# A hand-laid order for four engines in the opening of a gated mLSTM and differential-attention block, with in-bank output gates and the remainders of q and k on GpSimd

## The chip, the cores and the metric

The kernel runs on one core of one Trainium2 chip. The metric is the device time of one execution in microseconds (us). The median of three runs of the kernel before is 1762.96 us (1762.74 to 1768.04). A difference of about 0.3%, some 5 us, is what a measurement of this kernel can tell from none.

## The reference

One block over a sequence of 1024 tokens of width 1024, in fp32. The parts that matter here:

```python
h = rmsnorm(x, norm_g)
proj = h @ w_in                       # 11 segments of 1024 columns and one of 16
(a_q, a_k, a_v, a_o, a_z, a_g, b_q, b_k, b_v, b_z, g_a, g_b) = split(proj)
qk = silu(centred_depthwise_conv(concat(a_q, a_k), conv_w))     # 5 taps
h_fw, h_bw = mlstm(mq, mk, mv, gates from a_g), the same reversed
y_a = rmsnorm(h_fw + h_bw) * sigmoid(a_o) * silu(a_z)           # "output gates"
y_b = rmsnorm(diff_attention(rope(b_q), rope(b_k), b_v)) * silu(b_z)
mix = sigmoid(g_a + gb[0]) * (y_a @ w_branch_a) + sigmoid(g_b + gb[1]) * (y_b @ w_branch_b)
out = rmsnorm(x + mix @ w_out) * final_g
```

## The kernel before, in words

**Number format.** Every large product is made from two fp32r parts, a rounded high part `H` and a remainder `L = value - H`, with three matmuls (H·H, H·L, L·H). Making a pair of parts costs a copy on ScalarE (ACT) and a subtraction on VectorE (DVE) or GpSimd (POOL). TensorE (PE) has the most work of all engines.

**Opening** (from `begin`, L1417, to `leave("p0")`). Eight tiles of x (128 tokens by 1024) are loaded on the SP queue: x0 to x3, the raw weights of the first gate block, x4 to x7, the next weights. `load_small` (L442) loads `norm_g` and `gate_b` on ACT's queue; `gate_b` arrives transposed by the DMA, element by element, as `gbh` [128, 16]. `norm_x` (L486) makes the sum of squares on ACT (L491), the power -1/2 on POOL (L141), and on DVE the small steps around it (L138 to L145) and the scaling of the tile (L493). PE transposes x0 to x3 into eight PSUM banks (L130; two of tag `pj`, six of tag `T`). `split_h` makes `hH` (ACT, L537) and `hL` (DVE, L538). Then come gate blocks g0 to g3: each is a column block of 128 for two halves of the tokens, 24 matmuls of 128x512 per half (L408), finished by a tanh on ACT (`gt`, L761) that empties one of the two `pj` banks. Their weights are split by `load_w` (ACT L197, then eight POOL subtractions L200). Between them PE transposes x4 to x7 (`transpose_x`), and `first_part` (`f`, ACT L508) and `sums` (L510 to L525) make four sums of h blocks (`t`, `f` on DVE L516, L519 and POOL L520, L521) and their parts `TH` (ACT L524) and `TL` (DVE L525). The sums are operands of the next stage.

**Pairs.** Sixteen pairs of column blocks of w_in follow, alternately one of k or q (with the convolution) and one of the output gates a_o and a_z. A pair takes seven products f0 to f6 of 12 matmuls each instead of eight (L277); `load_form` makes the weight form of each product (POOL L233, L238, ACT L254, and the remainder L256 on DVE for f0, f4, f6, on POOL for the rest). Products land in `T` banks, of which there are six in turn; sums (`u`, L280) and the sinks on DVE free them. `conv_sink` adds the product into `cin` (L339), runs the five taps in a bank (L353, L355), tanh (`tz`, L356), silu (`y`, L358), the high part (ACT L361) and the remainder (DVE L364), and stores the parts. `oz_sink` adds the product into an SBUF tile `oz` (L314), takes tanh (L316, L319), multiplies the halves (L320), and at last multiplies the two tiles of 1024 columns (L325). The gates of the mLSTM (`gch`, DVE) and the rope angles (`wk`) are made beside pairs 1 to 8.

After the pairs (from 424 us on in the profile) come attention, the mLSTM and the output products. The change leaves the order of instructions there as it was.

**What sets the order.** PE keeps the order in which the program is written. For ACT, DVE, POOL and SP a scheduler fixes each engine's order when the kernel is built, from its own estimate of costs; on the chip each engine then runs its list strictly in order and waits at the first instruction that is not ready.

Of the kernel before, what the change touches and what calls it, by code (L numbers as in the profile page):

```python
# [109 lines left out]
class Block:  # L110
    def __init__(self, tc, A):
        self.tc, self.nc, self.A = tc, tc.nc, A
        nc = self.nc
        self.v, self.a, self.p, self.t, self.q = nc.vector, nc.scalar, nc.gpsimd, nc.tensor, nc.sync
        self.wt = {}
        self.raws = {}
        self.ml, self.opening, self.terms = False, True, {}
        for n in ("w1", "w2", "wy", "wr"):
            setattr(self, n, _Late(self, "_" + n))
        self.gc = {}  # L120
# [50 lines left out]
    def load_w(self, key):  # L171
        if key in self.wt:
            return
        if key[0] == "sw":
            return self.load_form(key)
# [83 lines left out]
    def pair_units(self, p, sink):  # L259
# [9 lines left out]
        def product(f, k0):  # L269
# [20 lines left out]
            elif f == 3:  # L290
                sink(1, 1, ps, box["u3"])
                add(box["u2"], box["u2"])
# [12 lines left out]
    def oz_sink(self, i0):  # L305

        v, a, box = self.v, self.a, {}

        def sink(i, j, ps, rest):
            if i not in box:  # L310
                box[i] = (self.big("oz"), [])
            t, got = box[i]
            c = slice(j * 512, (j + 1) * 512)
            v.tensor_tensor(out=t[:, c], in0=ps, in1=rest, op=ALU.add)  # L314
            if i == 0:
                a.activation(out=t[:, c], in_=t[:, c], func=AF.Tanh, scale=0.5)  # L316
            else:
                th = self.s0.tile([128, 512], F32, name="tz", tag="tz", bufs=2)
                a.activation(out=th, in_=t[:, c], func=AF.Tanh, scale=0.5)  # L319
                v.scalar_tensor_tensor(out=t[:, c], in0=th, scalar=1.0, in1=t[:, c], op0=ALU.add, op1=ALU.mult)  # L320
            got.append(j)
            if len(got) < 2 or len(box) < 2 or any(len(g) < 2 for _, g in box.values()):
                return
            o, z = box[0][0][:, 0:S], box[1][0][:, 0:S]
            v.scalar_tensor_tensor(out=z, in0=o, scalar=1.0, in1=z, op0=ALU.add, op1=ALU.mult)  # L325
            self.q.dma_start(out=self.gd_ml[i0], in_=z)
        return sink

    def conv_sink(self, seg, n):
# [3 lines left out]
        def sink(i, j, ps, rest):  # L333
# [12 lines left out]
            for half in range(2):  # L346
# [17 lines left out]
                v.tensor_tensor(out=lo.bitcast(F32R), in0=yh, in1=H, op=ALU.subtract)  # L364
# [3 lines left out]
    def run(self, units):  # L368
# [10 lines left out]
        for i, u in enumerate(units):  # L379
            if u.keys:  # L380
# [3 lines left out]
                while nxt < len(order) and (order[nxt][0] != "sw" or hasattr(self, "_s0")) and (nxt < need or nxt <= need + (4 if order[nxt][0] == "sw" else 1) and room(order[nxt])):  # L384
                    self.load_w(order[nxt])
                    nxt += 1
# [55 lines left out]
    def load_small(self, pool):  # L442
        A, q = self.A, self.a
        self.gin = pool.tile([8, 128], F32, name="gin")
        q.dma_start(out=self.gin, in_=A["norm_g"].rearrange("o (t c) -> (o t) c", c=128))
        self.gbh = self.const.tile([128, 16], F32, name="gbh")
        q.dma_start(out=self.gbh, in_=A["gate_b"].rearrange("o g (t c) -> c (o g t)", c=128))
# [13 lines left out]
    def norm_gain(self):  # L461
        ps = self.bank("T")
        self.tr(ps[:, 0:8], self.gin)
        self.g_in = self.const.tile([128, 8], F32, name="g_in")
        self.v.tensor_copy(self.g_in, ps[:, 0:8])

# [19 lines left out]
    def norm_x(self, pool, i):  # L486

        x = self.xs[i]
        ssq = pool.tile([128, 1], F32, name="ssqx", bufs=2)
        sq = pool.tile([128, D], F32, name="sq", tag="sq", bufs=2)  # L490
        self.a.activation(out=sq, in_=x, func=AF.Square, accum_out=ssq)  # L491
        rs = self.rsqrt(pool, ssq, 1.0 / D, EPS, f"rs{i}", bufs=2)
        self.v.tensor_scalar(out=x, in0=x, scalar1=rs[:, 0:1], scalar2=None, op0=ALU.mult)  # L493
# [16 lines left out]
    def sums(self, pool, k, half):  # L510

        v, p, fb = self.v, self.p, lambda x: x.bitcast(F32)
        f, ps, g = self.f[k], self.xps[k + 4 * half], self.g_in[:, k + 4 * half:k + 4 * half + 1]
        if half == 0:
            self.t12 = t = pool.tile([128, D], F32, name="t12", tag="sq", bufs=2)
            v.scalar_tensor_tensor(out=t[:, 0:512], in0=ps, scalar=g, in1=f[:, 0], op0=ALU.mult, op1=ALU.subtract)  # L516
            return
        t1, t2 = self.t12[:, 0:512], self.t12[:, 512:1024]
        v.scalar_tensor_tensor(out=t2, in0=ps, scalar=g, in1=t1, op0=ALU.mult, op1=ALU.subtract)  # L519
        p.tensor_tensor(out=f[:, 0], in0=t2, in1=f[:, 0], op=ALU.subtract)  # L520
        p.tensor_tensor(out=f[:, 1], in0=f[:, 1], in1=t2, op=ALU.subtract)  # L521
        t = (t1, t2, f[:, 0], f[:, 1])
        for i in (1, 0, 2, 3):
            self.a.copy(self.TH[i][:, k], t[i])  # L524
            v.tensor_tensor(out=self.TL[i][:, k], in0=t[i], in1=fb(self.TH[i][:, k]), op=ALU.subtract)  # L525
# [847 lines left out]
    def build(self):  # L1373
# [21 lines left out]
        with pool(name="const", bufs=1) as self.const, \  # L1395
                pool(name="dram", bufs=1, space=bass.MemoryType.DRAM) as self.dram, \
                pool(name="psA", bufs=1, space=bass.MemoryType.PSUM) as self.psA, \
                pool(name="wts", bufs=1) as wp, \
                tc.manual_schedule(engines={mybir.EngineType.PE}):
# [20 lines left out]
            def begin():  # L1420
# [4 lines left out]
                keys = [g[0].keys[0] for g in (g0, g1)]  # L1425
# [7 lines left out]
                for i in range(4):  # L1433
                    self.norm_x(self.p0, i)
                self.load_w(keys[0])
# [6 lines left out]
                  enter("p0", "p0", side="right"), banks("ps0", T=6), do(begin))  # L1442
# [4 lines left out]
            w.add(*[do(lambda i=i: self.transpose_block(i), 8 * TP) for i in range(4)])  # L1447
            first = lambda a, b: [self.first_part(self.p0, j) for j in range(a, b)]
# [116 lines left out]
```

## Time and profile before

| | value |
|---|---|
| median of three runs | 1762.96 us |
| the profiled execution's own time | 1767.53 us |
| its span, first to last instruction | 1765.8 us |
| PE busy | 1669.9 us (95%) |
| PE busy up to 86.52 us, where the pairs begin | 59.0 us |
| PE busy in the pairs, 86.52 to 424 us | 320.5 of 337.5 us |
| DVE, POOL busy in the pairs | 296.2 us, 177.1 us |
| granted TensorE clock: opening, pairs, the rest | 0.94, 0.97, 0.99 |

Time outside the span is 1.7 us. A granted clock of 0.94 over 86.5 us means that 0.06 of that stretch was lost to a slower clock. "Idle before" in a row is the time its engine stood still just ahead of it, and the name behind the arrow is what ended that.

### The profile page before, as it was taken

The numbers are of one execution on the slowest core, as the hardware profiler recorded it, in microseconds if no ns is written. First come the engines' busy times: TensorE is split into PE (matmuls) and PEld (weight loads), VectorE is DVE, ScalarE is ACT, GpSimd is POOL, SyncE is SP. The second block draws the span as 40 slices with busy tenths as digits, with TensorE's granted clock in tenths as the row PEclk, the third lists the DMA queues.
The fourth block names the chain that finished last, engine by engine and source line by source line (L and its number), as shares of the span: only waits on it lengthen the run. The fifth ranks groups of instructions, "written<-read, shape, count | busy, mean of one in ns | idle before, by whom it ended". The sixth has DMA issues, their size and how long they took to land. (4 is left out here: it accounts for less than half of the span.)

```text
span 1765.8 us, 24827 instructions
## 1 busy us (share of the span) xinstructions
PE 1669.9 (95%) x9119; PEld 1426.4 (81%) x9119; DVE 1064.3 (60%) x1957; ACT 769.9 (44%) x1522; POOL 568.6 (32%) x576
## 2 busy tenths in 40 slices
PE   4998998999999999999999989989999989999998
PEld 3777776788878888798789878889999877878886
DVE  3779989887156666666666755425666743225533
ACT  5544544444245554445445444424655643122211
POOL 3654654553331423312441331222321311222000
PEclk9999999999999999999999999999999989999999
DMA  5243434343634523451535162156454327344222
GB/s 153 84 130 103 137 108 131 108 143 120 145 94 108 142 62 82 126 134 43 145 94 132 47 151 67 61 158 188 136 163 148 100 75 251 122 140 134 84 84 84
DMA packets 191484, 208.15 MB, mean 118 GB/s; under 512 B 14681, under 2 KB 137954, under 8 KB 191362
## 3 DMA queue, kind: packets, MB, share of 16 engines
q1 hardware_dynamic: 188418, 204.98, 39.9%
q10 hardware_dynamic: 2944, 1.59, 0.3%
q8 instruction: 72, 1.18, 0.3%
q14 instruction: 50, 0.41, 0.1%
HBM read 143.47 MB, written 63.05 MB: 117 GB/s over the span
## 5 line engine op out<-in xcount | busy, mean ns | idle before, releaser
L408 PE MATMUL pj<-hH,wH 128*128 128x512 f32 x640 | 260.5, 407 | 14.4 <-ACT f L508 4.6
L408 PE MATMUL pj<-hH,wL 128*128 128x512 f32 x640 | 254.3, 397 | 0.1
L408 PE MATMUL pj<-hL,wH 128*128 128x512 f32 x640 | 253.8, 397 | 0.1
L853 ACT ACTIVATE e<-S,nm 128x1024 f32<-128x1024 f32 x128 | 143.1, 1118 | 179.1 <-DVE nm L851 178.8
L202 POOL TENSOR_TENSOR wL<-raw,wH 128x1024 fp32r<-128x1024 f32 x41 | 99.8, 2434 | 319.1 <-ACT wH L197 319.1
L874 DVE TENSOR_TENSOR pL<-T,pH 128x512 fp32r<-128x512 f32 x128 | 88.0, 687 | 139.9 <-ACT pH L873 139.8
L851 DVE TENSOR_REDUCE nm<-S 128x1 f32<-128x1024 f32 x128 | 155.8, 1217 | 20.2 <-PE S L849 20.0
L408 PEld LDWEIGHTS pj<-hH,wH 128*128 128x128 f32 x640 | 123.0, 192 | 38.9 <-ACT f L508 4.8
L430 PE MATMUL pj<-wH,hH 128*128 128x256 f32 x512 | 148.5, 290 | 0.2
L430 PE MATMUL pj<-wL,hH 128*128 128x256 f32 x512 | 145.9, 285 | 1.4 <-POOL wL L200 1.4
L430 PE MATMUL pj<-wH,hL 128*128 128x256 f32 x512 | 145.5, 284 | 0.0
L408 PEld LDWEIGHTS pj<-hH,wL 128*128 128x128 f32 x640 | 122.2, 191 | 27.9 <-POOL wL L187 0.9
L408 PEld LDWEIGHTS pj<-hL,wH 128*128 128x128 f32 x640 | 122.8, 192 | 23.4 <-DVE hL L538 0.6
L408 PE MATMUL pj<-sl_yb,wH 128*128 128x512 f32 x384 | 124.3, 403 | 4.1 <-ACT sl_yb L1258 2.0
L197 ACT CAST wH<-raw 128x1024 fp32r<-128x1024 f32 x56 | 58.7, 1052 | 125.3 <-PE pj L408 112.9
L430 PEld LDWEIGHTS pj<-wL,hH 128*128 128x128 f32 x512 | 98.5, 192 | 2.3 <-POOL wL L200 2.3
L430 PEld LDWEIGHTS pj<-wH,hH 128*128 128x128 f32 x512 | 98.7, 193 | 1.6 <-ACT wH L197 0.6
L430 PEld LDWEIGHTS pj<-wH,hL 128*128 128x128 f32 x512 | 98.5, 192 | 0.9
L355 DVE SCALAR_TENSOR_TENSOR T<-cin,cols,T 128x512 f32<-128x512 f32 x128 | 90.2, 752 | 7.3 <-ACT T L353 7.1
L849 PE MATMUL S<-kst,qH 128*128 128x512 f32 x256 | 89.7, 430 | 4.1 <-DMA kst<-stk 4.1
L860 DVE SCALAR_TENSOR_TENSOR e<-e,r,e 128x1024 f32<-128x1024 f32 x64 | 92.6, 1447 | 1.3
L408 PEld LDWEIGHTS pj<-sl_yb,wH 128*128 128x128 f32 x384 | 73.3, 191 | 24.5 <-DVE sl_yb L1259 3.2
(356 smaller groups left out, 4201.6 us busy)
## 6 DMA issues: line engine op xcount, KB each, us to landing
raw<-in_w_in_dram SPq DMA_DIRECT2D x88, 512.0 KB, 3.8
stk<-hl SPq DMA_DIRECT2D x64, 256.0 KB, 3.7
qH<-stk SPq DMA_DIRECT2D x32, 256.0 KB, 4.7
qL<-stk SPq DMA_DIRECT2D x32, 256.0 KB, 5.0
kst<-stk SPq DMA_DIRECT2D x16, 512.0 KB, 4.1
x<-in_x_dram SPq DMA_DIRECT2D x8, 512.0 KB, 3.8
cak<-y SPq DMA_DIRECT2D x16, 256.0 KB, 2.1
cakH<-cin SPq DMA_DIRECT2D x16, 256.0 KB, 2.0
```

The source lines that it names most:

```text
L197: self.a.copy(wH, raw)
L202: self.p.tensor_tensor(out=wL, in0=raw, in1=wHf, op=ALU.subtract)
L355: v.scalar_tensor_tensor(out=acc, in0=raw[:, o + x:o + x + 512], scalar=w(x), in1=acc, op0=ALU.mult, op1=ALU.add)
L408: self.t.matmul(ps, lhsT=l[:, k, :], rhs=r, start=(n == 0), stop=(n == 23))
L430: self.t.matmul(ps[:, i, :], lhsT=l, rhs=r[:, k, :], start=(kh == 0 and k == 0 and m == 0), stop=(kh == 1 and k == 3 and m == 2))
L849: self.t.matmul(ps[:, o], lhsT=x[:, j, c], rhs=st["k"][:, j, o], start=first, stop=not first)
L851: v.tensor_reduce(out=nm, in_=ps, axis=AX.X, op=ALU.max, negate=True)
L853: a.activation(out=e, in_=ps, func=AF.Exp, bias=nm[:, 0:1], accum_out=Z[:, j, t:t + 1])
L860: v.scalar_tensor_tensor(out=e0, in0=e, scalar=r[:, 0:1], in1=e0, op0=ALU.mult, op1=ALU.add)
L874: v.tensor_tensor(out=pL[:, :, s], in0=ps, in1=pH[:, :, s].bitcast(F32), op=ALU.subtract)
```

## The change

1. **Order.** `keep(PE, ACT, DVE, POOL)` holds all four engines to the written order from the start to the end of the opening; `keep(PE)` then hands ACT, DVE and POOL back to the scheduler. The units of the opening are written anew: the normalisation is cut into `norm_a` (squares, mean, power), `norm_b` (one Newton step, now two DVE instructions) and `norm_c` (scaling by two columns in one instruction), the sums into `sums_a`, `sums_b`, `sums_l`. Weight loads stand at fixed places (`ld`), and the look-ahead in `run` is off in the opening.
2. **gate_b.** It is loaded as 16 rows of 128 beside `norm_g` and turned by PE in the same transpose; the halving of `gbh` moves to `norm_gain`, just behind it.
3. **oz_sink.** The product is added in its PSUM bank, tanh reads the bank, and one SBUF tile `oz` per pair takes the product of the halves; each half is stored by itself.
4. **conv_sink.** The remainder of q and k (32 subtractions of 128x512) moves from DVE to POOL.

```diff
 def oz_sink (per product, i: 0 is a_o, 1 is a_z; j: half)
-            v.tensor_tensor(out=t[:, c], in0=ps, in1=rest, op=ALU.add)
+            v.tensor_tensor(out=ps, in0=ps, in1=rest, op=ALU.add)
+            more = lambda out, x, y: v.scalar_tensor_tensor(out=out, in0=x, scalar=1.0, in1=y, op0=ALU.add, op1=ALU.mult)
             if i == 0:
-                a.activation(out=t[:, c], in_=t[:, c], func=AF.Tanh, scale=0.5)
+                a.activation(out=z if first else ps, in_=ps, func=AF.Tanh, scale=0.5)
+                if not first:
+                    more(z, ps, z)
             else:
-                a.activation(out=th, in_=t[:, c], func=AF.Tanh, scale=0.5)
-                v.scalar_tensor_tensor(out=t[:, c], in0=th, scalar=1.0, in1=t[:, c], op0=ALU.add, op1=ALU.mult)
-            v.scalar_tensor_tensor(out=z, in0=o, scalar=1.0, in1=z, op0=ALU.add, op1=ALU.mult)
-            self.q.dma_start(out=self.gd_ml[i0], in_=z)
+                a.activation(out=th, in_=ps, func=AF.Tanh, scale=0.5)
+                more(z if first else ps, th, ps)
+                if not first:
+                    more(z, z, ps)
 def conv_sink
-                v.tensor_tensor(out=lo.bitcast(F32R), in0=yh, in1=H, op=ALU.subtract)
+                p.tensor_tensor(out=lo.bitcast(F32R), in0=yh, in1=H, op=ALU.subtract)
 def load_small
-        q.dma_start(out=self.gbh, in_=A["gate_b"].rearrange("o g (t c) -> c (o g t)", c=128))
+        q.dma_start(out=self.gin[8:24], in_=A["gate_b"].rearrange("o g (t c) -> (o g t) c", c=128))
 def build
-                tc.manual_schedule(engines={mybir.EngineType.PE}):
+            w.add(..., keep(E.PE, E.Activation, E.DVE, E.Pool), do(begin))
-            w.add(*g0[:k], *g1[:k], *[tx[i] for i in (0, 4, 1, 5, 2, 6)], sums[0])
-            w.add(*g2[:k], tx[3], tx[7], *g0[k:], do(lambda: (self.params(), self.lam(self.p0))), *[sums[i] for i in (1, 2, 3)])
-            w.add(*g1[k:], *g2[k:])
+            w.add(nA(0), nB(0), nC(0), tb(0), nA(1), nB(1), nA(2), nC(1), tb(1), nB(2), nA(3), nC(2), tb(2), nB(3), nC(3), tb(3))
+            w.add(ld(0), sp(0), fp(0), *[sp(i) for i in range(1, 8)], fp(1), nA(4), ld(1), nA(5), *g0[:k])
+            w.add(nB(4), nC(4), nA(6), nB(5), nC(5), nA(7), ld(2), fp(2, 3, 4, 5, 6, 7), nB(6), nC(6), nB(7), nC(7), *g1[:k])
+            w.add(*g2[:4], tx(0, 4, 1, 5), *g2[4:6], sA(0), tx(2, 6), *g2[6:k])
+            w.add(*g0[k:k + 4], tx(3, 7), sB((0, 1)), *g0[k + 4:k + 7], sB((0, 0)), sA(1), sL((0, 2), (0, 3)), g0[k + 7])
+            w.add(sB((1, 1), (1, 0)), sA(2), sL((1, 2), (1, 3)), ld(3), *g1[k:], sB((2, 1), (2, 0)), sA(3), sL((2, 2), (2, 3)))
+            w.add(*g2[k:], sB((3, 1), (3, 0)), sL((3, 2), (3, 3)), do(lambda: (self.params(), self.lam(self.p0))), keep(E.PE))
```

How the lists of three engines change at the places of which the prediction speaks. First DVE at the very start, before the change; `gbh` is the gate bias, `rs_v`, `rs_w`, `rs_y` the small columns of the normalisation, `x` a tile:

```order
L1415 MEMSET mhalf 128x8
L1451 TENSOR_SCALAR gbh<-gbh 128x16
L138 TENSOR_SCALAR rs_v<-ssqx 128x1 x2
L142 TENSOR_TENSOR rs_w<-rs_y 128x1 x2
L465 COPY g_in<-T 128x8
L143 TENSOR_TENSOR rs_w<-rs_w,rs_v 128x1 x2
```

The same place on DVE after the change:

```order
L1455 MEMSET mhalf 128x8
L473 COPY g_in<-T 128x8
L474 TENSOR_SCALAR gbh<-T 128x16
L502 TENSOR_SCALAR rsv<-ssqx 128x1
L509 SCALAR_TENSOR_TENSOR rsv<-rsy,rsv 128x1
L510 TENSOR_SCALAR rsv<-rsv 128x1
L514 TENSOR_SCALAR x_182<-x_182,rsy,rsv 128x1024
```

The halving of `gbh` stood at the head of DVE's list, ahead of all of the normalisation, and waited for the element-wise DMA; now the head waits for PE's transpose of 24 rows, and tile x0 is scaled before any other tile is begun.

Then ACT from the first split to the first tanh, before the change (`sq` are squares of x4 to x7, `f` the copies for the sums, `wH` high parts of weights):

```order
L491 ACTIVATE sq,ssqx<-x_200 128x1024
L491 ACTIVATE sq,ssqx<-x_202 128x1024
L508 ACTIVATE f<-T,g_in 128x512 x6
L197 CAST wH<-raw 128x1024 x2
L761 ACTIVATE gt<-pj,gbh 128x512
```

The same stretch of ACT after the change:

```order
L529 ACTIVATE f<-pj,g_in 128x512
L501 ACTIVATE sq,ssqx<-x_195 128x1024
L199 CAST wH<-raw 128x1024
L501 ACTIVATE sq,ssqx<-x_197 128x1024
L790 ACTIVATE gt<-pj,gbh 128x512
```

The weights of g1 now come behind one square instead of behind all squares and six copies `f`.

At last POOL in pair 0 (k) and pair 1, after the change; `tz` and `y` are the moved remainders, the rest makes weight forms:

```order
L240 TENSOR_TENSOR s1f<-raw 128x512
L369 TENSOR_TENSOR tz<-y,cin 128x512 x2
L258 TENSOR_TENSOR wH<-s2f,wH 128x512
L235 TENSOR_TENSOR s2f<-s1f,raw 128x512
L369 TENSOR_TENSOR tz<-y,cin 128x512 x2
L258 TENSOR_TENSOR wL<-s2f,wL 128x512
```

Before, the same list had no L369 rows; four subtractions that wait for DVE's `y` and ACT's copy now stand between the steps that make weight forms for PE.

123 lines of the change are left out of this document (73 added, 50 removed).

## The prediction

> **What bounds the kernel now.** I read the page first, then PE's waits up to the end of the pairs, then busy time by stretches, then the timeline around each wait.
>
> ```profile
> span 1765.8 us, 24827 instructions
> PE 1669.9 (95%) x9119; PEld 1426.4 (81%) x9119; DVE 1064.3 (60%) x1957; ACT 769.9 (44%) x1522; POOL 568.6 (32%) x576
> ```
>
> PE is the bound: 96 us of the span are all that a better order can win, besides time lost to a slow clock. Who ends PE's waits, up to 430 us (total, times, longest):
>
> ```profile
> PE pj L130 <- DVE x L493: 12.9, 1, 12.9
> PE T L277 <- DVE cin L339: 11.1, 3, 5.6
> PE pj L408 <- ACT f L508: 4.6, 1, 4.6
> PE pj L408 <- ACT gt L761: 3.9, 1, 3.9
> PE pj L408 <- ACT wH L197: 2.8, 1, 2.8
> PE T L277 <- DVE y L358: 2.2, 1, 2.2
> PE T L130 <- DVE y L358: 1.9, 1, 1.9
> PE T L277 <- DVE oz L314: 1.3, 1, 1.3
> ```
>
> Four waits are in the opening (24.2 us), the others in the pairs (16.5 us). The stretches show what a wait costs beyond itself:
>
> ```profile
> core 0: us, PE busy (x) PEld busy (x) DVE busy (x) ACT busy (x) POOL busy (x), PEclk, DMA share, GB/s
> 0.00:9.00 9.00, 0.24 (x1) 0.18 (x1) 0.07 (x1) 3.58 (x5) 0.94 (x7) 1.00 0.83 262
> 16.00:23.00 7.00, 5.87 (x32) 5.01 (x32) 4.46 (x15) 4.11 (x8) 6.27 (x11) 1.00 0.37 103
> 23.00:34.00 11.00, 7.20 (x24) 5.48 (x24) 9.27 (x28) 8.27 (x16) 1.66 (x3) 0.84 0.19 48
> 34.00:44.00 10.00, 7.22 (x25) 5.83 (x26) 1.63 (x6) 4.36 (x8) 6.72 (x16) 0.83 0.28 80
> 70.00:86.52 16.52, 12.64 (x48) 10.25 (x49) 8.80 (x6) 6.22 (x12) 15.73 (x15) 0.90 0.34 101
> 86.52:424.00 337.48, 320.45 (x1391) 259.21 (x1390) 296.19 (x447) 157.01 (x266) 177.13 (x151) 0.97 0.38 120
> 195.00:210.00 15.00, 12.80 (x50) 10.11 (x50) 14.84 (x27) 8.38 (x15) 3.14 (x4) 0.89 0.48 161
> 215.00:225.00 10.00, 8.65 (x45) 6.89 (x44) 9.63 (x20) 3.84 (x7) 8.79 (x10) 1.00 0.31 99
> ```
>
> After the 2.2 us wait (195 to 210) the clock averages 0.89: 0.11 × 15 = 1.7 us lost. After the 1.3 us wait (215 to 225) it stays 1.00. The waits of 4.6, 2.8 and 3.9 us cost 0.16 × 11 = 1.8, 0.17 × 10 = 1.7 and 0.10 × 16.5 = 1.7 us more. So a wait over 2 us costs its length and 1.7 us. [...]
>
> **The change part by part.** *The start.* Rows of the timeline (start, length, engine, operation, idle before and what ended it):
>
> ```profile
> 4.40 1.06 ACT L491 ACTIVATE sq<-x 128x1024 f32<-128x1024 f32 x1 [1.32 <-DMA x<-in_x_dram]
> 5.37 0.19 ACT L491 ACTIVATION_READ_ACCUMULATOR sq<-x 128x1 f32 x1
> 13.06 0.17 DVE L1451 TENSOR_SCALAR gbh<-gbh 128x16 f32<-128x16 f32 x1 [12.19 <-DMA gbh<-in_gate_b_dram]
> 16.03 0.69 PE L130 MATMUL pj<-ident,x 128*128 128x128 f32 x2 [12.86 <-DVE x L493]
> 24.37 0.56 POOL L141 TENSOR_TENSOR rs_y<-rs_v,mhalf 128x1 f32<-128x1 f32 x1 [1.70 <-DVE rs_v L138]
> 27.58 0.75 DVE L493 TENSOR_SCALAR x<-x,rs_y 128x1024 f32<-128x1024 f32 x1
> ```
>
> x0 is there at 4.40, but DVE stands at `gbh` until 13.06. With `gate_b` as 16 rows that wait goes. Then: square and its read to 5.6, mean 0.17 (as the small step on `gbh`), power 0.56, two more small steps of 0.17, scaling 0.75, and some 0.5 of hand-over between the engines (my estimate): PE begins at 7.9 instead of 16.03, **−8.1**. What is late next is x3: 262 GB/s over the first 9 us is 2.36 MB, so four tiles (2.1 MB) are in by 8.5, the first weights (2.6 MB) by about 10. Square of x3 to 9.9, and each further block adds 1.3 to 1.5 on DVE and PE: the four blocks end near 14 instead of 22.2 (32 transposes took 5.9 of busy time). That shift is the same 8.1; I add **+0.8** for DVE's pace between blocks. The 16 rows are no longer than the 8 rows of `norm_g` in kind; should they come at 7, the loss is 1.5.
>
> *Transposes to g0, g0 to g1.*
>
> ```profile
> 26.75 0.79 PE L408 MATMUL pj<-hH,wH 128*128 128x512 f32 x1 [4.59 <-ACT f L508]
> 28.25 3.38 DVE L538 SCALAR_TENSOR_TENSOR hL<-T,g_in,hH 128x512 fp32r<-128x512 f32 x5
> 32.19 3.60 ACT L508 ACTIVATE f<-T,g_in 128x512 f32<-128x512 f32 x6
> 35.61 2.06 ACT L197 CAST wH<-raw 128x1024 fp32r<-128x1024 f32 x2
> 36.78 0.80 PE L408 MATMUL pj<-hH,wH 128*128 128x512 f32 x1 [2.83 <-ACT wH L197]
> 36.80 6.72 POOL L200 TENSOR_TENSOR wL<-raw,wH 128x128 fp32r<-128x128 f32 x16 [3.34 <-ACT wH L197]
> ```
>
> g0 needs its bank: one split (ACT 0.6, DVE 3.38/5 = 0.68) and one `f` (3.60/6 = 0.6). These now stand first, and can begin when the last block's first transposes are in. The 4.59 becomes about 1, **−3.6**. From the first matmul of g0 to the first of g1 it took 36.78 − 26.75 = 10.0. Now ACT sets it: seven `hH` (4.2), one `f` (0.6), one square with its read (1.25), the cast (1.03), first POOL part (6.72/16 = 0.42): 7.5 from g0's start, **−2.5**. g0 itself took 7.2 with the slow clock (busy, 23 to 34) and would take 5.5 without, so the wait left is 0.3 to 2; I take the 1.7 behind 36.78 as saved, **−1.7**.
>
> *g2b to g3.*
>
> ```profile
> 72.62 0.62 ACT L524 CAST TH<-f 128x512 fp32r<-128x512 f32 x1 [1.05 <-POOL f L521]
> 73.15 0.68 ACT L761 ACTIVATE gt<-pj,gbh 128x512 f32<-128x512 f32 x1
> 73.88 0.50 PE L408 MATMUL pj<-hH,wH 128*128 128x512 f32 x1 [3.89 <-ACT gt L761]
> 66.22 1.76 POOL L520 TENSOR_TENSOR f<-t,f 128x512 f32<-128x512 f32 x1
> ```
>
> The tanh that frees g3's bank stood behind the `TH` copies of all four sums, which waited for POOL (1.76 each). Now g1b's tanh stands behind those of the third sum's `t` and one weight cast, and g2b's 24 matmuls (g0's 7.2 less 1.7 of clock: 5.5) cover it: by the same durations the bank is free some 2.5 ahead. **−3.9 and −1.7.** If POOL or DVE is over 2.5 late there, the difference returns as a wait. POOL's own list is later at its end: g3's remainders, two sums, then the forms of pair 0; by 1.7 apiece the form for f1 is ready about when PE asks, **+1** (0 to 3).
>
> Sum of the opening: −8.1 + 0.8 − 3.6 − 2.5 − 1.7 − 3.9 − 1.7 + 1 = −19.7, or −20. Four engines in a fixed order have many waits that this walk cannot see; I allow **+2**, most of one wait like the 2.83: **−18** (−8 if only the start holds, −23 if nothing is late).
>
> *The pairs.* PE's list is the same, so the lead is kept unless DVE, busy 296 of 337, falls behind.
>
> ```profile
> L364 DVE TENSOR_TENSOR tz<-y,cin x16: 669/685/1780, 109.1 to 385.5; 128x512 fp32r<-128x512 f32 x16
> L364 DVE TENSOR_TENSOR y<-y,cin x16: 669/686/1778, 162.8 to 423.9; 128x512 fp32r<-128x512 f32 x16
> L256 POOL TENSOR_TENSOR wL<-s2f,wL 128x512 fp32r<-128x512 f32 x12 | 16.9, 1408 | 50.6 <-ACT wL L254 50.6
> 260.57 0.50 PE L277 MATMUL T<-hH,wH 128*128 128x512 f32 x1
> 263.86 0.68 DVE L314 TENSOR_TENSOR oz<-T,u 128x512 f32<-128x512 f32 x1
> ```
>
> 32 subtractions of 0.69 leave DVE: 22 us over the pairs. PE gains only where DVE's backlog reaches a wait. The 1.3 wait follows a k convolution with four of them (2.7): **−1.3**. Ahead of the 5.6 wait DVE was 263.86 − 260.57 = 3.3 late, behind four more: **−2.6**, its clock loss stays. The other waits (11.1 − 5.6 = 5.5 for the other two on `cin`, 2.2 and 1.9) follow the gates' chain or the five taps of the same convolution, ahead of its subtractions; they stay. The output gates put the same elements through DVE in 8 instructions more, at most 8 × 0.69 = 5.5, off PE's path.
>
> On POOL the 32 cost 1.41 to 1.76 each: 45 to 56 on 177 busy of 337. The form behind which they stand waited 50.6/12 = 4.2 on average, so POOL has cover. DVE pays when both engines meet: the subtraction on DVE took 0.69 in the median and 1.78 at most, a bound of 1.1 for each meeting. I take **+0.9** (0 to 8 × 1.1 = 8.8). [...] Pairs: **−3** (−12 to +9).
>
> **The rivals.** *Only the start moves.* New in-order waits take the place of the three removed ones; for it speaks that ACT is full from the first split to g1. −8.1 and −1: 1754 on the median's scale. *The pairs gain as well:* a lighter DVE also dissolves the waits of 2.2 and 1.9, half of the 5.5, and two clock losses (−10): 1732; against it, taps and banks of a convolution are as before. *The lead is lost:* DVE, not PE, paces the pairs and they end where they did: 1760; against it, PE is 95% busy there (320 of 337). *Slower:* in the four k pairs the remainder is written into `tz`, which has two buffers; each is held until POOL's subtraction and its store are done, and POOL may stand before it at a form that waits for ACT. The third tanh then waits 4.2 + 1.76 = 6.0, behind it `y`, behind that the bank that PE wants, with 1.7 of clock: 7.7 × 4 = 31. It decides once a k pair loses over 21/4 = 5.2. 31 − 21 gives 1773. Against it: DVE's own pace puts the third tanh late anyway, after eight taps more.
>
> **How the numbers follow.** −18 − 3 = −21 from the profiled execution's own 1767.53 (1.7 outside its span) is 1746.5. That execution stood 4.6 above the median, so the median becomes 1742. Chances: forecast 0.67, only the start 0.13, pairs too 0.11, lead lost 0.05, slower 0.04. The range 1730 to 1754 holds the first three and leaves the last two. A difference of 0.3% is 5.3 us: faster 0.91, within 0.05, slower 0.04.
>
> **What would show it.** PE's first transpose of a tile near 8; g0's first matmul near 15, g1's near 22; no wait on `gt` before g3; the pairs begin 16 to 22 us earlier; in them the waits for `oz` gone, the longest for `cin` near 3, and the other `cin` waits still near 5. Wrong would be a start after 11, any wait of PE over 2 us in the opening behind the start, or PE waiting for a form of POOL or for `y` more than now.

## The result and the profile after

The kernel after took 1754.15 us (median of five runs, 1752.55 to 1756.33). The kernel before, in the same comparison, took 1766.75 (median of five, 1762.74 to 1768.04). The ratio is 0.9938, with a 95% interval of 0.9921 to 0.9955: faster, by 8 to 14 us. The prediction was 1742, with a range up to 1754, so it had the sign right; the gain of 21 us that it added up is 1.7 times the measured 12.6.

The page of the kernel after: PE is still busy 95% of the span, which is 13.4 us shorter (1765.8 before).

```profile
span 1752.4 us, 24818 instructions
PE 1668.2 (95%) x9119; PEld 1423.2 (81%) x9119; DVE 1037.9 (59%) x1917; ACT 767.4 (44%) x1522; POOL 603.2 (34%) x608
```

PE's waits of the kernel after up to 430 us (total, times, longest). The four long ones of the opening are gone; what is left ahead of the first transpose of a tile is 5.4 and 2.3 us, where 2.9 and 12.9 stood before. The lines that wait for `cin`, `y`, `oz` and `gc_negM` are in the pairs.

```profile
PE T L279 <- DVE cin L344: 11.0, 3, 5.5
PE T L131 <- DMA gin<-in_gate_b_dram: 5.4, 1, 5.4
PE pj L131 <- DVE rsv L502: 2.3, 1, 2.3
PE T L279 <- DVE y L363: 2.2, 1, 2.2
PE T L131 <- DVE y L363: 1.9, 1, 1.9
PE pj L416 <- POOL wL L202: 1.8, 2, 1.1
PE T L131 <- DVE oz L319: 1.6, 1, 1.6
PE pj L416 <- ACT f L529: 1.5, 1, 1.5
PE T L279 <- POOL wL L258: 1.3, 1, 1.3
PE T L279 <- DVE gc_negM L769: 0.6, 1, 0.6
```

The opening on the timeline of the kernel after: the first transpose of a tile came at 7.96 (16.03 before), g0 at 16.16 (26.75), g1 at 22.75 (36.78).

```profile
7.96 0.69 PE L131 MATMUL pj<-ident,x 128*128 128x128 f32 x2 [2.34 <-DVE rsv L502]
16.16 0.50 PE L416 MATMUL pj<-hH,wH 128*128 128x512 f32 x1 [1.52 <-ACT f L529]
22.75 0.49 PE L416 MATMUL pj<-hH,wH 128*128 128x512 f32 x1 [0.36 <-ACT wH L199]
```

Busy time of the kernel after by stretches (length, PE, PEld, DVE, ACT, POOL, granted clock, DMA share, GB/s): in the opening the clock is whole. In the pairs DVE has 274.88 us of work where it had 296.19, and POOL 215.64 where it had 177.13. PE's idle time there is 340.10 − 320.70 = 19.4 us; it was 337.48 − 320.45 = 17.0.

```profile
0.00:16.16 16.16, 6.92 (x34) 5.76 (x34) 6.19 (x20) 8.37 (x13) 8.66 (x21) 1.00 0.93 326
22.75:69.00 46.25, 44.46 (x209) 36.03 (x210) 36.83 (x52) 26.66 (x46) 31.64 (x38) 1.00 0.31 92
69.90:410.00 340.10, 320.70 (x1379) 258.59 (x1378) 274.88 (x424) 157.06 (x271) 215.64 (x189) 0.97 0.38 120
```

Where the time came from is read best from matmuls that stand at the same place in both of PE's lists. Before:

```profile
156.61 0.76 PE L277 MATMUL T<-hH,wL 128*128 128x512 f32 x1 [4.83 <-DVE cin L339]
199.12 0.50 PE L277 MATMUL T<-hH,wL 128*128 128x512 f32 x1 [2.20 <-DVE y L358]
222.11 0.50 PE L277 MATMUL T<-hH,wH 128*128 128x512 f32 x1 [1.35 <-DVE oz L314]
286.06 0.77 PE L277 MATMUL T<-hH,wL 128*128 128x512 f32 x1 [5.62 <-DVE cin L339]
329.43 0.66 PE L130 MATMUL T<-ident,rep 128*128 128x128 f32 x4 [1.88 <-DVE y L358]
```

And the same five after:

```profile
139.88 0.77 PE L279 MATMUL T<-hH,wL 128*128 128x512 f32 x1 [4.81 <-DVE cin L344]
182.50 0.50 PE L279 MATMUL T<-hH,wL 128*128 128x512 f32 x1 [2.20 <-DVE y L363]
206.63 0.47 PE L279 MATMUL T<-hH,wH 128*128 128x512 f32 x1 [0.64 <-DVE gc_negM L769]
271.85 0.76 PE L279 MATMUL T<-hH,wL 128*128 128x512 f32 x1 [5.53 <-DVE cin L344]
315.46 0.66 PE L131 MATMUL T<-ident,rep 128*128 128x128 f32 x4 [1.88 <-DVE y L363]
```

The lead (how much earlier the same matmul starts after the change) is 16.7, 16.6, 15.5, 14.2 and 14.0 us, and 13.4 at the end. So the opening, counted up to the first of these waits, won 16.7 (forecast 18), and the pairs, which were to win 3, lost 2.7. Nearly all of that loss lies on both sides of the third row, the place in pair 6 where PE takes up the columns of the mLSTM gates. I call it "the columns" below.

### The profile page after: what moved, and what is told of

It reads as the page before. It is cut to its first block, busy times and chain, and to the rows that moved or that the text cites. A ratio compares the mean times of both kernels' runs of the same rounds, so it can differ in the third digit from the quotient of the medians.

```text
span 1752.4 us, 24818 instructions
## 1 busy us (share of the span) xinstructions
PE 1668.2 (95%) x9119; PEld 1423.2 (81%) x9119; DVE 1037.9 (59%) x1917; ACT 767.4 (44%) x1522; POOL 603.2 (34%) x608
## 5 line engine op out<-in xcount | busy, mean ns | idle before, releaser
L416 PEld LDWEIGHTS pj<-hL,wH 128*128 128x128 f32 x640 | 121.4, 190 | 23.4 <-DVE hL L567 0.6
L416 PEld LDWEIGHTS pj<-sl_yb,wH 128*128 128x128 f32 x384 | 73.3, 191 | 25.3 <-DVE sl_yb L1288 3.3
```

The lines of the kernel that those rows point to most:

```text
L416: self.t.matmul(ps, lhsT=l[:, k, :], rhs=r, start=(n == 0), stop=(n == 23))
```

## The experiments

All times are compared with runs of the kernel before on the same chip. Three questions were open: what in the opening won, why the pairs lost, and whether the waits left in the pairs can be moved away.

One piece of the change is easy to miss. In product f3 of every pair, DVE's step that makes `u2` now stands ahead of the sink; before, it stood behind it.

```diff
             elif f == 3:
+                add(box["u2"], box["u2"])
                 sink(1, 1, ps, box["u3"])
-                add(box["u2"], box["u2"])
```

The runs below that undo the output gates leave this as it is, and the runs that put the new output gates into the kernel before bring it along. No run tried it apart.

**The opening: the order without the rows.** The order by hand stays; `gate_b` is gathered element by element again, and the halving stands late on DVE.

```diff
-        q.dma_start(out=self.gin[8:24], in_=A["gate_b"].rearrange("o g (t c) -> (o g t) c", c=128))
+        q.dma_start(out=self.gbh, in_=A["gate_b"].rearrange("o g (t c) -> c (o g t)", c=128))
...
-            w.add(nB(4), ..., nB(7), nC(7), *g1[:k])
+            w.add(nB(4), ..., nB(7), nC(7), do(lambda: self.v.tensor_scalar(out=self.gbh, in0=self.gbh, ...)), *g1[:k])
```

> The kernel after, but gate_b is again gathered element by element, and DVE's halving of it stands behind the last of the eight tiles' scaling, ahead of g1, where the gather has landed long before. Theory (the rows win only because DVE stood at the halving in the order of before): the first transpose of a tile comes within 1 us of 8, g0 within 1 us of 16.2, and the lead at the pairs' start is 15 to 17 us as in the kernel after; ratio 0.992 to 0.996. Rival (the gather itself, 2,048 elements, holds the DMA engines and delays tiles and weights): the first transpose after 9 or g0 after 18, the lead 3 to 8 us smaller, ratio 0.996 to 0.999.

Measured: 1751.55 (1750.73 to 1758.70), ratio 0.9929 (0.991 to 0.9948). The first transpose of a tile and g0 on its timeline:

```profile
7.69 0.69 PE L131 MATMUL pj<-ident,x 128*128 128x128 f32 x2 [4.92 <-DVE rsv L501]
15.97 0.50 PE L416 MATMUL pj<-hH,wH 128*128 128x512 f32 x1 [1.52 <-ACT f L528]
```

Both come slightly earlier than in the kernel after. The gather still takes 12 us from issue to landing, but nobody stands behind it. The theory holds, the rival falls: with the order, the rows are worth nothing that shows.

**The opening: the rows without the order.** The kernel before, with `gate_b` loaded as 16 rows, transposed by PE, and halved on the way out of PSUM.

```diff
+        q.dma_start(out=self.gin[8:24], in_=A["gate_b"].rearrange("o g (t c) -> (o g t) c", c=128))
...
+        self.v.tensor_scalar(out=self.gbh, in0=ps[:, 8:24], scalar1=0.5, scalar2=None, op0=ALU.mult)
...
-            w.add(do(lambda: (first(2, 8), half())))
+            w.add(do(lambda: first(2, 8)))
```

> The kernel before, with gate_b loaded as rows and turned by PE, and nothing else; the scheduler orders the engines. If the element-wise DMA at the head of DVE's list was the whole of the late start: PE's first transpose of a tile near 8 to 9, about 7.5 us faster, about 1758. If the hand order is needed for it as well (tile by tile): first transpose near 11 to 12, 3 to 4 us faster. The waits of 4.6, 2.8 and 3.9 later in the opening stay in either case.

Measured: 1759.82 (1758.64 to 1762.61), ratio 0.996 (0.9946 to 0.9974).

```profile
10.10 0.69 PE L130 MATMUL pj<-ident,x 128*128 128x128 f32 x2 [4.44 <-DVE x L494]
20.83 0.79 PE L408 MATMUL pj<-hH,wH 128*128 128x512 f32 x1 [4.99 <-ACT f L509]
67.96 0.52 PE L408 MATMUL pj<-hH,wH 128*128 128x512 f32 x1 [3.92 <-ACT gt L762]
```

The start moves by 5.9, to 10.10; in the old order DVE still does other things ahead of x0's scaling. That lies between the two expectations (8 to 9, and 11 to 12); the time is the first one's. The waits of 4.99 and 3.92 (4.59 and 3.89 before) stay, and so does the lead: 156.61 − 150.68 = 5.9 at the first long `cin` wait. So rows and order remove the same wait at the start, and the order alone removes the other three. The order is one bundle here: which of its moves removes which of the three was not tried apart.

**The order and the rows, both edits of the pairs undone** (all but the new place of `u2`).

```diff
-                p.tensor_tensor(out=lo.bitcast(F32R), in0=yh, in1=H, op=ALU.subtract)
+                v.tensor_tensor(out=lo.bitcast(F32R), in0=yh, in1=H, op=ALU.subtract)
...
-            v.tensor_tensor(out=ps, in0=ps, in1=rest, op=ALU.add)
+            v.tensor_tensor(out=t[:, c], in0=ps, in1=rest, op=ALU.add)
...
```

(The rest of the second piece is the output gates' function of before.)

> The change, with both edits of the pairs undone: the hand order of the opening and the rows of gate_b alone. If the pairs' edits are worth nothing or less: 16 to 17 us below the kernel before, about 1750, the pairs' waits as in the kernel before (17 us idle) and the lead at their beginning kept to the end. If the pairs' edits help: slower than the change, 1756 or more.

Measured: 1755.81 (1754.04 to 1757.30), ratio 0.9934 (0.9921 to 0.9947). That is the kernel after within the scatter: the edits of the pairs add nothing that shows to the new opening. But the 1750 that was expected for edits worth nothing did not come either, since PE's waits did not go back to those of before: the columns' waits are 1.97 and 0.93, the longest `cin` wait is 6.00, and the lead there is 286.06 − 273.95 = 12.1 (the traced execution is the longest of the five).

**One edit of the pairs undone.** First the remainder back on DVE:

```diff
-                p.tensor_tensor(out=lo.bitcast(F32R), in0=yh, in1=H, op=ALU.subtract)
+                v.tensor_tensor(out=lo.bitcast(F32R), in0=yh, in1=H, op=ALU.subtract)
```

> The change, with the 32 remainders of q and k back on DVE. Three theories of why the pairs gained nothing (PE idle 19.4 us there against 17.0 before, though DVE is 21 us lighter). Bursts: PE's long waits come from DVE's serial chains (gates, angles) and a convolution's own banks, not from DVE's total load: within 2 us of the change (1754), the 5.5 and 4.8 waits stay. Payback: POOL's subtractions stretch DVE's small SBUF steps beside them, and that made the wait at the gates' columns 1.57 + 0.64 with a clock loss: 2.5 us faster, about 1751.5. Load (my forecast's): 4 us slower, about 1758, the waits for cin and for oz longer by 1 to 3.

Measured: 1756.38 (1749.51 to 1759.66), ratio 0.9935 (0.9913 to 0.9957); longest `cin` wait 5.57, waits at the columns 1.26, 0.86 and 0.63. The payback theory, by which the columns' wait would go, falls. Then the output gates as before, remainders on GpSimd:

```diff
-            v.tensor_tensor(out=ps, in0=ps, in1=rest, op=ALU.add)
+            v.tensor_tensor(out=t[:, c], in0=ps, in1=rest, op=ALU.add)
...
-                self.q.dma_start(out=self.gd_ml[i0][:, j * 512:(j + 1) * 512], in_=z)
+            self.q.dma_start(out=self.gd_ml[i0], in_=z)
```

> The change, with the output gates as before (added into SBUF tiles). Banks: the in-bank gates hold a T bank until tanh and product are done, and that made the wait ahead of the gates' columns (1.57, released by oz) and the clock loss behind it: 2.6 us faster, about 1751.5, the wait for oz at most 1.35 and the clock 1.00 behind it. Payback or bursts: within 1 us of the change, the wait stays. Load: also within 1 us, since the elements are the same.

Measured: 1757.31 (1749.19 to 1759.99), ratio 0.9939 (0.992 to 0.9957); the waits at the columns are 0.20, 1.11 and 1.43 (the traced execution is the longest of the six). Neither undoing gives or takes anything that can be measured, and the wait at the columns doesn't go with the banks.

**The edits of the pairs alone, in the opening of before.** This is the opposite direction, and it was needed: with a new opening the wait at the columns was there whatever was undone in the pairs.

```diff
-                v.tensor_tensor(out=lo.bitcast(F32R), in0=yh, in1=H, op=ALU.subtract)
+                p.tensor_tensor(out=lo.bitcast(F32R), in0=yh, in1=H, op=ALU.subtract)
...
-            v.tensor_tensor(out=t[:, c], in0=ps, in1=rest, op=ALU.add)
+            v.tensor_tensor(out=ps, in0=ps, in1=rest, op=ALU.add)
...
```

(The rest is that of the output gates, with the new place of `u2`.)

> The kernel before, with the two edits of the pairs alone: output gates made in banks, remainders of q and k on GpSimd. The opening is that of before. Theory (bursts): the waits of 1.3, 4.8 and 5.6 us in the pairs stay within 0.7 us each, the time is that of the kernel before, ratio 0.998 to 1.002. The prediction's own step for the pairs: the wait for oz gone and the longest for cin near 3, 3 us faster, ratio 0.998, or 0.996 with a clock spell saved. Rival (contention of DVE and GpSimd costs): 1.002 to 1.005.

Measured: 1772.33 (1768.22 to 1774.76, twelve runs), ratio 1.0026 (1.0016 to 1.0037): 5 us slower. The prediction's −3 for the pairs falls, and so does my theory that they are worth nothing; the ratio is the contention rival's. Each edit alone followed, first the remainders on GpSimd:

```diff
-                v.tensor_tensor(out=lo.bitcast(F32R), in0=yh, in1=H, op=ALU.subtract)
+                p.tensor_tensor(out=lo.bitcast(F32R), in0=yh, in1=H, op=ALU.subtract)
```

> The kernel before, with only the remainders of q and k moved to GpSimd (opening, output gates as before). Theory (DVE's small steps on SBUF alone stretch from 0.3 to 1.4 us while GpSimd works, so the moved work comes back to DVE where its chain is serial): the seven steps of the gates' weights take about 7 us in place of 3.9, the wait ahead of the gates' columns grows from 1.35 to 2.5 or more with a clock spell behind it, the longest cin wait stays 5.5: 3 to 5 us slower than the kernel before, ratio 1.0015 to 1.003. Rival (the prediction's step): the seven steps as in the kernel before, the longest cin wait near 3, ratio 0.997 to 0.999.

Measured: 1769.16 (1765.57 to 1774.39), ratio 1.0015 (1.0005 to 1.0026): at the lower end of what the theory gave, with its longer steps and columns' wait (below), and a longest `cin` wait of 5.85. Then the output gates in banks, with the new place of `u2`:

```diff
-            v.tensor_tensor(out=t[:, c], in0=ps, in1=rest, op=ALU.add)
+            v.tensor_tensor(out=ps, in0=ps, in1=rest, op=ALU.add)
...
-            self.q.dma_start(out=self.gd_ml[i0], in_=z)
+                self.q.dma_start(out=self.gd_ml[i0][:, j * 512:(j + 1) * 512], in_=z)
```

> The kernel before, with only the output gates made in banks (remainders on DVE). Theory (the 5 us that both edits of the pairs cost come from GpSimd's subtractions): the seven steps of the gates' weights take 4 us as in the kernel before, waits in the pairs within 0.7 us of it, ratio 0.999 to 1.001. Rival (the banks are held through two instructions of ScalarE and DVE more, so that PE waits for a bank): the waits ahead of the gates' columns add up to 2.5 us or more with a clock spell behind them, ratio 1.0015 to 1.003.

Measured: 1769.89 (1767.19 to 1773.07), ratio 1.0021 (1.001 to 1.0031). The theory that GpSimd's subtractions are the whole cost falls; the rival's ratio and its waits at the columns came. Whether the banks do it or the new place of `u2` is not shown, and the traced execution is the longest of the twelve (1773.07). Each of the two costs is only 2 to 4 us, and its interval only just excludes no change at all.

The steps on `gch` (the gates' weights, on DVE) show what the lighter DVE did. Last steps of before:

```profile
208.91 0.14 DVE L716 COPY gch<-T 64x1 f32<-64x1 f32 x1
215.56 0.28 DVE L726 TENSOR_SCALAR gch<-gch 64x256 f32<-64x256 f32 x1
215.76 0.21 DVE L731 COPY gch<-gch 64x128 f32<-64x128 f32 x1
```

The same three with only the remainders on GpSimd:

```profile
206.76 0.14 DVE L716 COPY gch<-T 64x1 f32<-64x1 f32 x1
213.73 1.37 DVE L726 TENSOR_SCALAR gch<-gch 64x256 f32<-64x256 f32 x1
215.03 1.33 DVE L731 COPY gch<-gch 64x128 f32<-64x128 f32 x1
```

Counted from the matmul behind the 2.2 us wait for `y` (199.12 before, 198.92 here), the chain begins 9.79 behind it before and 7.84 here: the subtractions that left DVE did bring 1.95 us. But the chain lasts 7.06 before (208.91 to 215.97) and 9.60 here (206.76 to 216.36): 2.5 are given back. Four steps that read and write SBUF alone take 1.33 to 1.40 each; before, one of them took 1.39 too, but the others 0.80, 0.28 and 0.21. All nine steps of the chain add up to 7.2 us in place of 3.9. The kernel after shows the same, begun 7.83 behind its matmul and lasting 9.62; there the four long steps (1.40, 1.38, 1.38 and 1.33, begun at 194.70, 196.02, 197.32 and 198.62) stand beside four instructions of GpSimd (2.16, 1.34, 1.34 and 1.36, begun at 193.79, 195.91, 197.21 and 198.51). I read this as a matter of which steps meet, which no busy total shows.

What DVE's steps meet is mostly not the moved work. The run without any remainder (below) has only weight forms on POOL in this stretch; its chain, too, begins 7.84 behind the matmul (183.41), and it lasts 9.09. Its first and last step:

```profile
191.25 0.14 DVE L745 COPY gch<-T 64x1 f32<-64x1 f32 x1
198.90 1.44 DVE L760 COPY gch<-gch 64x128 f32<-64x128 f32 x1
```

So about 2.0 of the 2.5 come back because the steps, being earlier, meet forms that GpSimd made before the change as well; the subtractions on GpSimd add 0.5. In the three runs that have them on DVE and the new place of `u2`, the chain lasts 7.03 to 7.05.

At the columns PE then waits longer than before, and the clock goes down behind it. Stretches of 14 us, begun 4 to 6 ahead of the columns' last wait, with the granted clock in the third column from the end; in this order: before, after, pairs alone, remainders alone, banks alone.

```profile
218.00:232.00 14.00, 12.65 (x63) 10.19 (x62) 10.51 (x21) 5.91 (x10) 6.49 (x9) 1.00 0.38 114
```

```profile
202.00:216.00 14.00, 11.80 (x50) 9.27 (x49) 8.20 (x20) 5.45 (x10) 5.43 (x4) 0.88 0.40 114
```

```profile
218.00:232.00 14.00, 10.51 (x40) 7.96 (x39) 8.04 (x20) 4.83 (x9) 6.02 (x9) 0.76 0.26 77
```

```profile
217.00:231.00 14.00, 10.53 (x40) 8.05 (x39) 9.42 (x19) 5.06 (x9) 5.88 (x9) 0.76 0.24 77
```

```profile
218.00:232.00 14.00, 11.35 (x42) 8.63 (x41) 8.29 (x21) 4.42 (x8) 6.24 (x9) 0.76 0.29 90
```

The waits there add up to 1.35, 2.21, 3.49, 3.47 and 2.65 us. The clock lost is nothing, 0.12 × 14 = 1.7 and three times 0.24 × 14 = 3.4. From the first long `cin` wait to the second PE took 286.06 − 156.61 = 129.5 before, and 129.7 with only the rows, whose wait there is 1.35 too. The kernel after took 132.0, the three with edits of the pairs in the old opening 133.1, 133.2 and 132.6, and the one with the new order and the old pairs (but for `u2`) 133.3. So the old order with the old pairs is the one arrangement in which the stretch between these waits cost so little. Each other arrangement of the whole computation with the angles in their place took 2 to 4 us more (up to 1.4 of it ahead of the wait for `y`).

The sum of the waits alone misleads here, because it depends on the clock ahead of it. Behind the 2.2 us wait for `y` the kernels before and after lost 1.7 us of clock (before: the prediction's row from 195 to 210, at 0.89). Behind the same wait of 2.25 us, the run with only the remainders on GpSimd lost nothing:

```profile
194.90:209.90 15.00, 12.75 (x57) 10.24 (x56) 14.90 (x26) 9.46 (x17) 6.24 (x6) 1.00 0.48 151
```

Its PE comes to the columns so much sooner and waits for DVE so much longer. Counted from the matmul behind the wait for `y` to the matmul behind the columns' last wait, the way takes 23.0 to 23.4 us in the five kernels that have the subtractions on DVE (22.99 before). With them on GpSimd it takes 24.0 to 24.1 in six kernels, 23.2 in the one with the output gates of before, and 25.3 in the one that has the angles beside it. So the moved subtractions and their longer chain mostly go with columns that come up to 1 us later; the exception, at 23.2, has the longer chain too (9.56). The rest of what is lost lies behind the columns, where the clock goes down, and that happened with the short chain as well (the banks alone). What decides it there was not found.

**No remainder at all.** The subtraction is left out on both engines, and the high part stands in for the remainder (this part of the computation is changed).

```diff
-                p.tensor_tensor(out=lo.bitcast(F32R), in0=yh, in1=H, op=ALU.subtract)
+                lo = H
```

> The kernel after, without the subtraction that makes the remainders of q and k in the convolutions: the high part is stored in the remainder's place (this part of the computation is changed), so neither DVE nor GpSimd has the 32 instructions. Theory (PE's waits in the pairs are bursts of a few microseconds in which DVE's or ScalarE's own chain is serial, so the mean load does not matter): DVE stays near 275 us busy in the pairs, GpSimd falls by 38 us to about 177, the waits of 4.8, 2.2, 5.5 and 1.9 us stay, the time is within 4 us of the kernel after. Rival (GpSimd's subtractions slow DVE's small operations and that ate the gain): the waits at the columns and at the longest cin shrink by 2 us or more together and the time is 4 to 8 us below the kernel after, 0.989 to 0.991 of the kernel before.

Measured: 1752.41 (1741.75 to 1756.66), ratio 0.9914 (0.9891 to 0.9937), within 4 us of the kernel after as the theory had it, and with the rival's sign; the longest `cin` wait is shorter (5.53 after):

```profile
270.00 0.77 PE L279 MATMUL T<-hH,wL 128*128 128x512 f32 x1 [3.75 <-DVE cin L344]
```

So with the subtractions on neither engine this wait is 1.8 us shorter; with them on DVE (5.57) and on GpSimd (5.53) it is the same. Two steps of the angles ahead of it, in the kernel after:

```profile
L615 DVE TENSOR_SCALAR wk<-wk x1: 1414/1414/1414, 256.0 to 256.0; 128x256 f32<-128x256 f32 x1
L616 DVE TENSOR_SCALAR wk<-wk x1: 1382/1382/1382, 257.9 to 257.9; 128x256 f32<-128x256 f32 x1
```

And without any subtraction:

```profile
L615 DVE TENSOR_SCALAR wk<-wk x1: 287/287/287, 254.5 to 254.5; 128x256 f32<-128x256 f32 x1
L616 DVE TENSOR_SCALAR wk<-wk x1: 286/286/286, 255.3 to 255.3; 128x256 f32<-128x256 f32 x1
```

These two alone differ by 2.2 us. It is tempting to book that on the moved subtractions, but with the subtractions back on DVE the steps are just as long:

```profile
L615 DVE TENSOR_SCALAR wk<-wk x1: 1393/1393/1393, 256.6 to 256.6; 128x256 f32<-128x256 f32 x1
L616 DVE TENSOR_SCALAR wk<-wk x1: 1378/1378/1378, 258.5 to 258.5; 128x256 f32<-128x256 f32 x1
```

What POOL does beside them in the kernel after is again weight forms:

```profile
255.96 1.31 POOL L258 TENSOR_TENSOR wH<-s2f,wH 128x512 fp32r<-128x512 f32 x1 [2.41 <-ACT wH L256]
257.35 1.83 POOL L235 TENSOR_TENSOR s2f<-raw,s2f 128x512 f32<-128x512 f32 x1
```

Without the subtractions other steps stretch in their place: from the copy that begins the angles (`an`, L603, at 250.81 in the kernel after and at 249.35 without) to the matmul behind the wait it is 21.04 and 20.65 us. Most of the 1.8 is that the copy comes earlier, 16.9 ahead of the moment at which PE stops, in place of 15.5. Two DVE steps between the taps and that copy (L258, at 240.12 and 248.09) take 1.46 and 1.60 in the kernel after, 0.68 and 0.69 without. The first stands beside a moved subtraction, the second beside a form to which POOL came 1.7 us later than without the subtractions. My theory that the load doesn't matter is too strong: the load counts, and on GpSimd it holds DVE back by about as much as it relieved it. The columns' waits (0.81, 1.56 and 0.64) stay even here.

**Moving the angles away.** If the 5.5 us wait is a serial burst of DVE and ScalarE, it should go when the burst is moved beside a pair of output gates. Three kernels tried it: the angles one pair later, angles and tables later, and angles and tables earlier.

```diff
-            more = {..., 6: [columns], 7: [do(self.angle_loads)], 8: [do(self.angles)], 10: tab[0:2], 11: tab[2:4]}
+            more = {..., 6: [columns], 8: [do(self.angle_loads)], 9: [do(self.angles)], 10: tab[0:2], 11: tab[2:4]}
```

> The kernel after, with the loads for the rotary angles and the angles themselves moved one pair later (from pairs 7 and 8 to 8 and 9), so that the 2.5 us copies on DVE fall into a pair of output gates, whose convolutions make no conv inputs from DVE's taps. Theory (bursts): the 5.5 us wait for cin is gone, with the 3.4 to 6.8 us of half clock behind it (1.7 to 3.4 us lost): 7 to 9 us faster than the kernel after, about 1746, ratio to the kernel before 0.988 to 0.990. Rival (the wait is DVE's backlog and moves to the next convolution, where the tables follow at once): a wait of 3 us or more at another cin or y, time within 3 us of the kernel after, ratio 0.992 to 0.995.

Measured: 1765.09 (1756.76 to 1770.03), ratio 0.9984 (0.997 to 0.9998), where the kernel after has 0.9938: some 8 us of the gain are lost. The 5.5 is gone, and the transposes of the tables wait instead:

```profile
299.05 1.33 PE L131 MATMUL T<-ident,rep 128*128 128x128 f32 x5 [9.34 <-DVE rep L630]
```

```diff
+            more = {..., 8: [do(self.angle_loads)], 9: [do(self.angles)], 11: tab[0:2], 12: tab[2:4]}
```

> The kernel after, angles in pair 9 and their tables in pairs 11 and 12 (after: 8, 10 and 11), so that PE has a whole pair of convolutions between the angles' chain and the transposes that need it. Theory (bursts; a serial chain on DVE and ScalarE costs PE what the work placed between lacks): the 9.3 us wait of the run with the angles alone moved is gone, the longest cin wait falls from 5.5 to about 2.2, with one or two clock units saved: 3 to 6 us faster than the kernel after, ratio 0.990 to 0.992. Rival (the chain delays the conv inputs of pair 10 in the same way): a cin wait of 4 us or more behind pair 9, ratio 0.993 to 0.995.

Measured: 1760.44 (1756.95 to 1766.51), ratio 0.9964 (0.9953 to 0.9976).

```diff
+            more = {..., 6: [columns, do(self.angle_loads)], 7: [do(self.angles)], 9: tab[0:2], 10: tab[2:4]}
```

> The kernel after, with the angles' loads, the angles and their tables one pair earlier (6, 7, 9 and 10), so that the angles' chain lies beside the output gates of pair 7. Theory (bursts): as in the run with angles and tables later, 3 to 6 us faster than the kernel after, ratio 0.990 to 0.992, with the first conv input of pair 8 no longer behind the 2.5 us copies. Rival (the chain of pair 7 comes so soon behind the gates' columns that DVE is late for both): the wait at the columns or at pair 8's cin stays above 4 us, ratio 0.993 to 0.996.

Measured: 1757.59 (1755.43 to 1764.73), ratio 0.9954 (0.9936 to 0.9971). In these two PE waits for a bank of the output gates. Its tanh stands on ScalarE behind the angles' own steps, which wait for DVE's chain, and behind two table loads (1.28 each in the kernel after, at 255.90 and 272.45). First the later place, then the earlier:

```profile
301.21 0.80 PE L279 MATMUL T<-TH,wH 128*128 128x512 f32 x1 [6.04 <-ACT oz L321]
```

```profile
262.51 0.63 PE L279 MATMUL T<-TH,wH 128*128 128x512 f32 x1 [4.98 <-ACT oz L321]
```

All three expectations of a gain failed. In all three places a wait went with the chain: the output gates stand behind it as the convolutions did. The rivals of the first two named other places than those that took the wait; the third one's came in part, since the columns' waits of the earlier place add up to 4.7 (1.41, 2.77 and 0.54). No kernel tried that computes the reference is shown to be faster than the kernel after.

## Why the prediction was off

- *The start, −8.1:* right (16.03 − 7.96 = 8.07), but not by the edit that it was put down to. It is the halving's place on DVE that decides; the rows matter only in the old order. The 0.5 of hand-over was an estimate with no row of before behind it; in the kernel after, x0's seven instructions add up to 3.13 of the 3.66 us from 4.30 to 7.96, which leaves 0.53.
- *+0.8, −3.6, −2.5, −1.7:* together −15.1 up to g1, measured 36.78 − 22.75 = 14.0. g1 waited 0.36.
- *−3.9, −1.7, +1, +2:* the wait for `gt` went, and its clock loss too; the form in pair 0 cost 1.3 and a wait of 0.5 ahead of it. The lead grew from 14.0 to 16.7, forecast −2.6. The opening came to −16.7 for −18.
- *The pairs, −3: the step that failed.* It took DVE's 22 us of relief (21.3 came) to shorten two waits. "−1.3" for the wait on `oz`: in its place stand 2.2 us and 1.7 of clock. "−2.6" for the longest `cin` wait: 5.53 for 5.62. The relief reached the beginning of DVE's chains (1.95 us earlier ahead of the columns) and not their ends. "+0.9" for DVE and POOL holding each other up was the mis-sized term, and no run shows 0.9: I priced it by the subtraction's own rows (0.69 in the median, at most 1.78), and not by DVE's short steps on SBUF, which took up to 1.1 more each beside GpSimd (1.38 for 0.28), 3.3 in one chain, and which met weight forms as well once they came earlier. Ahead of the columns 2.5 were taken back where the relief was 1.95; at the `cin` wait the 1.8 that leaving the subtractions out brings did not come by moving them. My own row of before (215 to 225, clock 1.00 behind the 1.3 wait) should have warned me: a wait that is just short enough is a place to lose, since lengthening it cost clock as well (waits of 1.35 in all lost none, 2.21 lost 1.7 us, 3.49 lost 3.4).
- *"A wait over 2 us costs its length and 1.7 us":* too simple. The same wait of 2.2 us for `y` lost 1.7 us of clock in five kernels and nothing in nine. Of the terms priced by it, the opening's came, since its waits went.
- *The rival that the pairs gain as well* falls with it. "The lead is lost" is true in small: DVE, not PE, paces the stretch up to the columns, which takes 23 to 24 us whether PE's clock was down in it or not. The slower rival through `tz` didn't come: GpSimd's subtractions took 1.33 on average, and PE waited no longer for `y`.
- *The step to the median, −4.6:* the three runs of before had a median of 1762.96; with five it is 1766.75, and 29 runs beside the last experiments gave 1767.16. The profiled execution (1767.53) was an ordinary one, and subtracting 4.6 was wrong by about 4.

In all: 1.3 in the opening, 5.7 in the pairs, 0.6 later and 4.6 by that last step make the 12 us between 1742 and 1754.

What stays open: the edits of the pairs cost 5 us in the old opening (ratio 1.0016 to 1.0037) and nothing that shows in the new one (0.9938 with them, 0.9934 without). The second pair of numbers is uncertain by some 3 to 4 us, and the run without them keeps the new place of `u2`; so neither that the cost differs between the openings nor that the new order alone makes the columns late (2.9 us of waiting there) is shown. A rival was not tested either: the scheduler lays DVE's list at the columns anew in these kernels (with only the remainders moved, a step of L320 stands ahead of one of L314 that it followed before). Which of DVE's and POOL's meetings matter wasn't tried apart, since each needs another list of both engines.

## What to carry to other kernels

Price work that is moved to GpSimd by the short SBUF-to-SBUF steps of DVE that will then meet GpSimd's work, the old as well as the new (here 0.28 us became 1.38 to 1.41), and not by either engine's busy total. Before crediting a removed wait, look at the waits that are just short of costing clock (here 1.35 us, at a clock of 1.00): a change that only shifts two engines against each other can lose more there than it wins elsewhere. A cause is not settled by undoing an edit alone: here the edits of the pairs showed their cost only when they were put on the old kernel, and the undoing left one of their lines in place. A long step beside a moved one proves nothing until the same step is read in a run without the move.

## What the runs showed of the hardware

- At the columns the clock's losses come in units: stretches of 14 us around the waits lose nothing, 1.7 or 3.4 us. Waits that add up to 1.35 lost no unit in two kernels, 2.2 lost one in three, and 2.6 to 3.5 lost one in three kernels and two in five. The length alone doesn't decide: the wait of 2.2 us for `y` lost one unit in five kernels (clock 0.89 over 15 us) and none in nine (1.00). Behind that wait in the kernel before the clock reads 0.50 from 200.70 to 203.25, and 0.92 and 0.57 over the 0.85 us on either side: 1.7 us lost, as 3.4 us at 0.50 would lose.
- One and the same kernel (no remainder) took 1741.75 at a mean clock of 0.991 and 1756.66 at 0.983. A difference of 0.008 over 1750 us is 14 us, so nearly all of this scatter is clock. The median of the kernel before moved by 4 us from three executions to 29; medians of three are worth little below that.
- A DVE step of 0.28 us on 64x256 or 128x256 values took 1.38 to 1.41 beside a GpSimd instruction of about 1.3: L755 took 0.28 with the subtractions back on DVE and 1.38 in the kernel after (at 197.32, beside 1.34 at 197.21), L615 took 0.29 with no subtraction and 1.41 in the kernel after (at 256.00, beside 1.31 at 255.96). Not every meeting did this: before, the step of 0.28 at 215.56 stayed short beside an instruction of 2.16 begun at 215.57.
